# A two-layer decoder on one Trainium2 core: expert pieces of 896 columns, and expert rows given back by an indirect DMA

## Chip, cores and metric

The kernel runs on one core of a Trainium2 chip. The metric is the device time of one execution in microseconds; beside it the profiler gives the span of one profiled execution, from its first to its last instruction. The engines are TensorE (PE), VectorE (DVE), ScalarE (ACT), GpSimd (POOL) and SyncE (SP, which here only issues DMAs).

## What is computed

256 tokens of width 1024 go through two layers and a final RMSNorm, all in float32.

```python
for i in range(2):
    h = rmsnorm(x, norm_mix[i])                 # layer 0: S5 scan + GLU; layer 1: RWKV-7
    ca = memory_cross_attn(q, rmsnorm(mem, norm_mem[i]), w_kv_mem[i])
    x = x + concat([mix, ca]) @ w_out[i]
    h2 = rmsnorm(x, norm_ffn[i])
    x = x + (swiglu(h2, ...) if i == 0 else moe_swiglu(h2, ...))
return rmsnorm(x, norm_final)
```

The change concerns `moe_swiglu`, which takes about six tenths of the time. Each token picks its two best of eight experts; an expert is `(silu(h @ w_gate) * (h @ w_up)) @ w_down` with 1024 x 3584, 1024 x 3584 and 3584 x 1024 weights; its rows are scaled by the softmax weight of the choice and added to the token. Every expert's weights are read once: 8 x 44 MB of the 423 MB that the kernel moves.

## The kernel before, in words

**Products.** A float32 product is made of three fp32r products (`mm3`, L191 to L195): high part of x by high part of w, high by low, low by high. Each weight tile is therefore split on the chip (`split`, L173): ACT casts it to its high part (L187), DVE subtracts that to get the low part (L188), into a pool of four pairs (`ws`). The first expert's first pieces have their subtraction on GpSimd (L185).

**Weights.** `wload` (L119) fills a ring of seven tiles of 128 x 4096 floats, all through SP's queue (L63) in the order in which they are used. A tile is loaded again when its last split is done.

**Order.** The kernel writes its operations in program order and a scheduler places them on each engine by a simulated timeline; each engine, and SP's queue, then runs its list strictly in that order. A DMA that waits holds up every later DMA of SP.

**Experts.** Tokens are packed per expert into at most 128 rows; a second pass for fuller experts stands in a branch (L1757 to L1759) that these inputs don't take. `Gather` (L1445) builds a one-hot matrix `Gm` (tokens x rows) and gets the expert's rows by matmuls (L1458), turns them to columns (`xe`), and `back` (L1473) turns `Gm` into `GT` and fetches each row's weight and rstd (`wsl`). An expert's 3584 columns are cut into seven pieces of 512, so there are 56 jobs (expert, piece). A job runs 48 gate products into one PSUM tile `gu` of 128 x 512 (L193 to L195), then `between`: the previous job's activation is transposed and split (`act_T`, `ath` L1658 and `atl` L1659), and a finished expert is combined; then 48 up products, Silu on ACT (L1649) and the product with up on DVE (L1650). At piece 3 the next expert's rows are gathered. Last the previous job's down product runs, 24 products into two PSUM tiles `yac` that stay for the whole expert.

**Combine** (L1677). ACT scales `yac` by the rows' weights into a high part (L1685), DVE makes the low part (L1686), eight 128 x 512 products with `GT` (L1691, L1692) spread the rows to the tokens, and DVE adds them to the residual stream `xs` (L1696). For the last expert the adds go through `resid` (L269, L270), which also sums the squares for the final norm.

**Start.** The S5 stage loads its parameters (`bnat`, `cnat`, `gnat`) by SP among w_in_a's and mem's loads; PE transposes c (L507), ACT copies it (L514), makes U and Um (L537, L540) and the block columns BC (L501).

**End.** After the branch: `rstd_of` (L276 to L278), the scaling by rs and the gain `nfin` (L1766), and four stores. `nfin` was loaded on ACT's queue ahead of the experts (L1624 to L1626).

## Time and profile before

| | |
|---|---|
| median of 3 runs | 1589.86 us (1589.8 to 1590.88) |
| the profiled execution: time, span | 1590.0 us, 1588.0 us |
| mean granted clock of PE | 0.978 |
| busy: PE, DVE, ACT, POOL | 1516.3, 1283.0, 1073.0, 157.7 us |
| DMA packets, bytes | 198031, 423.46 MB |
| first gate product of the experts | 589.59 us |
| last down product | 1572.86 us |

How to read it: a row of the groups gives line, engine, operation, output tile and inputs, shapes and count, then busy time and mean nanoseconds of one, then the engine's idle time before it and what ended that. A row of the timeline gives start, duration, and in brackets the idle time before it. A row of the waits says who waited for whom, how long in total, how often, and the longest. Successive matmuls overlap in the profile, so that the distance of their starts, and not their duration, is what one costs in a stream. PSUM tiles and weight tiles carry the program's names.

### The profile page before, as it was taken

The page shows a single profiled execution, that of the slowest core. Times are in us where ns is not written, and L with a number is a line of the kernel's source. Part 1 is how long each engine was busy: PE and PEld are TensorE (multiplying, and loading weights), DVE is VectorE, ACT ScalarE, POOL GpSimd, SP SyncE. Part 2 cuts the span into 40 slices and gives each one's busy share as a digit, 9 for nine tenths or more (in the row PEclk, how much of TensorE's full clock was granted, in tenths as well). Part 3 has the DMA queues.
Part 4 walks back from the last instruction along what each step waited for, and adds up shares of the span by engine and source line. Part 5 has one row for each costly group of instructions (what it writes and reads, how often), then busy time and mean ns, then how long its engine had stood idle before and what let it go on. Part 6 is the DMA issues. An engine that isn't in the chain of part 4 may idle for free. (4 is left out here: it accounts for less than half of the span.)

```text
span 1588.0 us, 21853 instructions
## 1 busy us (share of the span) xinstructions
PE 1516.3 (95%) x8465; PEld 1272.1 (80%) x8465; DVE 1283.0 (81%) x1583; ACT 1073.0 (68%) x1355; POOL 157.7 (10%) x215
## 2 busy tenths in 40 slices
PE   7898999998969889999999999999999999999996
PEld 6776888878958768888888888888888888888885
DVE  7964654546895669899899899899899898988987
ACT  6655544436533348788777777787787887777775
POOL 3451000003652230000000000000000000000000
PEclk9999999999989979999999999999999999999999
DMA  7116553623400958999999999999999999999970
GB/s 202 45 45 237 185 203 117 248 79 94 120 14 22 339 218 313 341 371 359 346 374 353 344 376 356 340 378 356 347 372 363 348 366 361 352 348 366 360 280 29
DMA packets 198031, 423.46 MB, mean 267 GB/s; under 512 B 13952, under 2 KB 35614, under 8 KB 197918
## 3 DMA queue, kind: packets, MB, share of 16 engines
q1 hardware_dynamic: 195746, 419.29, 72.8%
q10 hardware_dynamic: 2172, 2.68, 0.6%
q8 instruction: 68, 1.11, 0.3%
q14 instruction: 45, 0.37, 0.1%
HBM read 420.91 MB, written 1.05 MB: 266 GB/s over the span
## 5 line engine op out<-in xcount | busy, mean ns | idle before, releaser
L188 DVE TENSOR_TENSOR wsl<-w,wsh 128x1024 fp32r<-128x1024 f32 (+1 forms) x757 | 893.8, 1216 | 150.9 <-ACT wsh L187 139.8
L187 ACT CAST wsh<-w 128x1024 fp32r<-128x1024 f32 (+1 forms) x757 | 783.3, 1049 | 250.9 <-PE gu L195 97.1
L194 PE MATMUL gu<-wsl,xeh 128*128 128x512 f32 x896 | 350.7, 391 | 0.0
L193 PE MATMUL gu<-wsh,xeh 128*128 128x512 f32 x896 | 348.9, 396 | 1.6 <-DVE xs L1696 1.6
L195 PE MATMUL gu<-wsh,xel 128*128 128x512 f32 x896 | 349.5, 390 | 0.0
L193 PEld LDWEIGHTS gu<-wsh,xeh 128*128 128x128 f32 x896 | 168.8, 188 | 37.4 <-ACT wsh L187 2.4
L195 PEld LDWEIGHTS gu<-wsh,xel 128*128 128x128 f32 x896 | 168.6, 188 | 35.1 <-DVE xel L1471 0.2
L194 PEld LDWEIGHTS gu<-wsl,xeh 128*128 128x128 f32 x896 | 168.7, 188 | 35.0
L194 PE MATMUL yac<-wsl,ath 128*128 128x512 f32 x440 | 173.0, 393 | 0.0
L195 PE MATMUL yac<-wsh,atl 128*128 128x512 f32 x440 | 171.7, 390 | 0.0
L193 PE MATMUL yac<-wsh,ath 128*128 128x512 f32 x440 | 136.3, 391 | 0.0
L278 POOL TENSOR_TENSOR rs<-vv,mhalf 128x1 f32<-128x1 f32 x8 | 4.4, 557 | 1203.6 <-DVE vv L277 1203.6
L195 PEld LDWEIGHTS yac<-wsh,atl 128*128 128x128 f32 x440 | 82.7, 188 | 17.1
L193 PEld LDWEIGHTS yac<-wsh,ath 128*128 128x128 f32 x440 | 82.2, 188 | 16.9
L194 PEld LDWEIGHTS yac<-wsl,ath 128*128 128x128 f32 x440 | 82.8, 188 | 15.4
L193 PE MATMUL mm<-wsh,hTh 128*128 128x512 f32 (+1 forms) x192 | 71.1, 374 | 0.0
L194 PE MATMUL mm<-wsl,hTh 128*128 128x512 f32 (+1 forms) x192 | 70.8, 371 | 0.0
L195 PE MATMUL mm<-wsh,hTl 128*128 128x512 f32 (+1 forms) x192 | 70.3, 372 | 0.0
L1658 ACT CAST ath<-t 128x512 fp32r<-128x512 f32 x55 | 32.3, 587 | 31.0 <-PE yac L194 30.2
L1650 DVE TENSOR_TENSOR sg<-sg,gu 128x512 f32<-128x512 f32 x56 | 38.1, 681 | 13.7 <-PE gu L195 13.7
L195 PE MATMUL dn<-hTh,wsC 128*128 128x256 f32 x160 | 46.5, 291 | 1.0 <-POOL wsC L1148 0.9
L193 PE MATMUL dn<-hTh,wsC 128*128 128x256 f32 x160 | 46.1, 288 | 0.0
(533 smaller groups left out, 2059.1 us busy)
## 6 DMA issues: line engine op xcount, KB each, us to landing
w<-in_moe_w_gate_dram SPq DMA_DIRECT2D x55, 2048.0 KB
w<-in_moe_w_up_dram SPq DMA_DIRECT2D x55, 2048.0 KB
w<-in_moe_w_down_dram SPq DMA_DIRECT2D x54, 2048.0 KB
w<-in_w_in_b_dram SPq DMA_DIRECT2D x22, 512.0 KB
w<-in_ffn_w_gate_dram SPq DMA_DIRECT2D x5, 2048.0 KB
w<-in_ffn_w_up_dram SPq DMA_DIRECT2D x5, 2048.0 KB
w<-in_ffn_w_down_dram SPq DMA_DIRECT2D x5, 2048.0 KB
w<-in_w_out_dram SPq DMA_DIRECT2D x4, 2048.0 KB
```

The costliest lines, as they stand in the source:

```text
L187: S.copy(hv, src)
L188: (eng or V).tensor_sub(lv, src, hv.bitcast(F32))
L193: TE.matmul(ps, xp[0], wh, start=start, stop=False, skip_group_check=True)
L194: TE.matmul(ps, xp[0], wl, start=False, stop=False, skip_group_check=True)
L195: TE.matmul(ps, xp[1], wh, start=False, stop=stop, skip_group_check=True)
L278: hold.append(G.tensor_tensor(rs, vv, mhalf, op=OP.pow).ins)
L1650: V.tensor_mul(sg, sg, ps[1])
L1658: S.copy(at[0], t)
```

## The change

**Expert pieces.** 896 columns in place of 512, so four pieces an expert and 32 jobs. Gate and up are loaded as two tiles of 128 x 4 x 896 each, down as one of four and one of three rows of 1024; runs in memory are 3584 bytes for gate and up (2048 before) and 4096 for down as before. Gate and up run in two halves of 448 columns, each with its own PSUM tile, so a job takes all four `gu` tiles; Silu, product and transposes follow those shapes, with one `sg` tile in place of two. The next expert's rows are gathered at piece 2.

**Giving back.** For the first seven experts ACT scales both halves of `yac` into one tile `ye`, and GpSimd scatters its 128 rows by an indirect DMA into a scratch `yd` in device memory: 512 rows, one for each token and rank of choice. The row number comes with the weights as a third column of `wt`, read in `back`; rows that hold no token fall outside and are skipped. GT, its transposes and the eight products remain for the last expert alone. During the last expert four reads of `yd`, each into `ye`, and four adds to `xs` on DVE (`added`) bring the rows in. `ye` has one buffer, also used for the gathered rows and by the last combine. `yd` is zeroed at the start by four DMAs from a cleared tile.

**Final norm.** `nfin` is loaded into a ring tile on ACT's queue after the branch.

**What moves.** On SP at the start, before (waits in brackets, `_49` belongs to the semaphores' names):

```order
L63 DMA srow2_111<-in_s5_d_dram 6x128 [waits DMAHW2_49]
L63 DMA srow2_111<-in_s5_b_glu_dram 6x128 [waits DMAHW3_49]
L63 DMA bnat_143<-in_s5_b_re_dram 128x24x16 [waits DMAHW4_49]
L63 DMA bnat_143<-in_s5_b_im_dram 128x24x16 [waits DMAHW5_49]
L63 DMA cnat_300<-in_s5_c_re_dram 128x6x64 [waits DMAHW6_49]
L63 DMA cnat_300<-in_s5_c_im_dram 128x6x64 [waits DMAHW7_49]
L63 DMA gnat_104<-in_s5_w_glu_dram 128x6x16 [waits DMAHW0_49]
```

and now:

```order
L63 DMA srow2_113<-in_s5_d_dram 6x128 [waits DMAHW2_49]
L63 DMA srow2_113<-in_s5_b_glu_dram 6x128 [waits DMAHW3_49]
L63 DMA yd_67<-KD_105 128x1024 [waits DMAHW4_49,Pool_49]
L63 DMA yd_67<-KD_105 128x1024 [waits DMAHW5_49]
L63 DMA yd_67<-KD_105 128x1024 [waits DMAHW6_49]
L63 DMA yd_67<-KD_105 128x1024 [waits DMAHW7_49]
L63 DMA bnat_149<-in_s5_b_re_dram 128x24x16 [waits DMAHW0_49]
L63 DMA bnat_149<-in_s5_b_im_dram 128x24x16 [waits DMAHW1_49]
L63 DMA cnat_306<-in_s5_c_re_dram 128x6x64 [waits DMAHW2_49]
L63 DMA cnat_306<-in_s5_c_im_dram 128x6x64 [waits DMAHW3_49]
L63 DMA gnat_106<-in_s5_w_glu_dram 128x6x16 [waits DMAHW4_49]
```

The four writes of zeros, which wait for GpSimd's clearing, stand ahead of every parameter of S5.

On DVE at the end, from the splits of the last down tile to the first residual add, before (`wsl` is the low part of a split, `w_22117` the last weight tile):

```order
L188 TENSOR_TENSOR wsl_22108<-w_21969,wsh_22107 128x1024 [waits DMAHW7_49,Activation_49]
L188 TENSOR_TENSOR wsl_22123<-w_22117,wsh_22122 128x1024 [waits DMAHW0_49,Activation_49]
L188 TENSOR_TENSOR wsl_22127<-w_22117,wsh_22126 128x1024 [waits DMAHW1_49,Activation_49]
L188 TENSOR_TENSOR wsl_22131<-w_22117,wsh_22130 128x1024 [waits DMAHW2_49,Activation_49]
L1659 TENSOR_TENSOR xel_22074<-t_22068,xeh_22073 128x512 [waits Activation_49]
L188 TENSOR_TENSOR wsl_22135<-w_22117,wsh_22134 128x1024 [waits DMAHW3_49,Activation_49]
L1686 SCALAR_TENSOR_TENSOR yel_22163<-yac_21357,wsl_20631,yeh_22162 128x512 [waits Activation_49]
L1686 SCALAR_TENSOR_TENSOR atl_22167<-yac_21358,wsl_20631,ath_22166 128x512 [waits Activation_49]
L269 TENSOR_TENSOR xs_72<-xs_72,gu_22170 128x512 [waits PE_49]
```

and now (`w_14226` and `w_14231` are the last two weight tiles, `yac_13584` the first half):

```order
L189 TENSOR_TENSOR wsl_14256<-w_14226,wsh_14255 128x1024 [waits DMAHW1_49,Activation_49]
L189 TENSOR_TENSOR wsl_14266<-w_14226,wsh_14265 128x1024 [waits DMAHW2_49,Activation_49]
L1655 TENSOR_TENSOR xs_74<-xs_74,ye_13581 128x1024 [waits DMAHW3_49]
L189 TENSOR_TENSOR wsl_14276<-w_14231,wsh_14275 128x1024 [waits DMAHW4_49,Activation_49]
L189 TENSOR_TENSOR wsl_14280<-w_14231,wsh_14279 128x1024 [waits DMAHW5_49,Activation_49]
L189 TENSOR_TENSOR wsl_14284<-w_14231,wsh_14283 128x1024 [waits DMAHW6_49,Activation_49]
L1655 TENSOR_TENSOR xs_74<-xs_74,ye_13852 128x1024 [waits DMAHW7_49]
L1726 SCALAR_TENSOR_TENSOR atl_14309<-yac_13585,wsl_12770,ath_14308 128x512 [waits Activation_49]
L1655 TENSOR_TENSOR xs_74<-xs_74,ye_13855 128x1024 [waits DMAHW0_49,DVE_49]
L1726 SCALAR_TENSOR_TENSOR ye_14305<-yac_13584,wsl_12770,ye_14305 128x512 [waits DMASW6_49,Activation_49]
L270 TENSOR_TENSOR xs_74<-xs_74,gu_14317 128x512 [waits PE_49]
```

The last three of the four adds (the rows onto `xs_74` from a `ye`) now stand among the last splits and ahead of the scaling of each half; the first stands 32 rows earlier.

On SP at the same place, now:

```order
L63 DMA w_14226<-in_moe_w_down_dram 128x1024 [waits DMAHW1_49]
L63 DMA w_14226<-in_moe_w_down_dram 128x1024 [waits DMAHW2_49]
L63 DMA ye_13581<-yd_67 128x1024 [waits DMAHW3_49,DVE_49]
L63 DMA w_14231<-in_moe_w_down_dram 128x1024 [waits DMAHW4_49,DVE_49]
L63 DMA w_14231<-in_moe_w_down_dram 128x1024 [waits DMAHW5_49]
L63 DMA w_14231<-in_moe_w_down_dram 128x1024 [waits DMAHW6_49]
L63 DMA ye_13852<-yd_67 128x1024 [waits DMAHW7_49,DMAHW3_49,DVE_49]
L63 DMA ye_13855<-yd_67 128x1024 [waits DMAHW7_49,DMAHW0_49,DVE_49]
L1802 COMPARE_AND_BRANCH
```

The third and the fourth read each wait for DVE, that is for the add before, since all go into the one `ye`; before, the last row here ahead of the branch was a load of weights.

The diff:

```diff
-    pad(consts, 64)
...
+    dr = pool(ctx, "dr", 1, space=bass.MemoryType.DRAM)
+    yd = dr.tile([2 * T, D], F32, name="yd")
...
+        for i in range(2 * NH):
+            dma(yd[i * P:(i + 1) * P, :], KD_[:, 0:2].rearrange("p q d c -> p (q d c)"))
...
-    wt = mcon.tile([P, NH, E, 2], F32, name="wt")
+    wt = mcon.tile([P, NH, E, 4], F32, name="wt")
+    tok = mcon.tile([P, NH], F32, name="tok")
...
+    pad(mcon, 96)
     class Gather:
...
-        def back(self, tr):
-
-            self.GT = self.mp.tile([P, NH, P], F32R, name="GT")
+        def back(self, tr, turned):
+
...
+            if turned:
+                self.GT = self.mp.tile([P, NH, P], F32R, name="GT")
+                for h in range(NH):
+                    TE.transpose(t[:, h, :], self.Gm[:, h, :].bitcast(F32), ident)
...
-                TE.transpose(t[:, h, :], self.Gm[:, h, :].bitcast(F32), ident)
-            for h in range(NH):
-                TE.matmul(t[:, 2, 0:2], self.Gm[:, h, :].bitcast(F32), wt[:, h, e, :], start=h == 0, stop=h == NH - 1,
+                TE.matmul(t[:, 2, 0:3], self.Gm[:, h, :].bitcast(F32), wt[:, h, e, 0:3], start=h == 0, stop=h == NH - 1,
...
-            S.copy(self.GT, t[:, 0:2, :])
+            if turned:
+                S.copy(self.GT, t[:, 0:2, :])
...
+            self.place = smk([P, 1], I32, "it")
+            V.tensor_scalar(self.place, t[:, 2, 2:3], 2.0 * T, None, op0=OP.add)
...
+        G.iota(tok, pattern=[[P, NH]], base=0, channel_multiplier=1, allow_small_or_imprecise_dtypes=True)
...
+        V.tensor_scalar(wt[:, :, :, 2], rkk, float(T), -2.0 * T, op0=OP.mult, op1=OP.add)
+        V.tensor_add(wt[:, :, :, 2], wt[:, :, :, 2], tok[:, :, None].to_broadcast([P, NH, E]))
...
-    NCK = FE // 512
+    CW = 896
+    NCK, KW, HW = FE // CW, CW // P, CW // 2
     def tr():
...
     def gu():
...
-    nfin = mp.tile([P, D], F32, name="nfin", bufs=1)
-    ap = a["norm_final"]
-    dma(nfin, bass.AP(tensor=ap.tensor, offset=ap.offset, ap=[[0, P], [1, D]]), S)
+    def ye_tile():
+        return mp.tile([P, D], F32R, name="ye", tag="ye", bufs=1)
+
+    def halved(t):
+        return lambda q: t[:, q * 512:(q + 1) * 512].bitcast(F32)
     def gather(e, base):
...
-        g.columns(lambda q: mp.tile([P, 512], F32R, name="xr", tag="ye" + "hl"[q], bufs=1).bitcast(F32))
-        g.back(tr)
+        g.columns(halved(ye_tile()))
+        g.back(tr, base > 0 or e == E - 1)
...
+
+    def added(k, h):
+
+        b = ye_tile().bitcast(F32)
+        dma(b, yd[k * T + h * P:k * T + (h + 1) * P, :])
+        V.tensor_add(xs[:, h, :], xs[:, h, :], b)
     def gate_up(g, w_in, between, first):
...
-            w = w_in[nm]
-            p_ = gu()
-            for wh, wl, k0 in split(ws, w, 4, last=hold if first and nm == "gate" else None):
-                for j in range(2):
-                    k = k0 + j
-                    mm3(p_, (g.xe[0][:, k, :], g.xe[1][:, k, :]), wh[:, j, :], wl[:, j, :], k == 0, k == KD - 1)
-            ps.append(p_)
+            ps += [gu() for _ in range(2)]
+            for i, w in enumerate(w_in[nm]):
+                for wh, wl, k0 in split(ws, w, 4, last=hold if first and nm == "gate" and i == 0 else None):
+                    k = 4 * i + k0
+                    for n in range(2):
+                        ns = slice(n * HW, (n + 1) * HW)
+                        mm3(ps[-2 + n][:, :HW], (g.xe[0][:, k, :], g.xe[1][:, k, :]), wh[:, 0, ns], wl[:, 0, ns], k == 0,
+                            k == KD - 1)
...
-        sg = mp.tile([P, 512], F32, name="sg")
-        S.activation(sg, ps[0], AF.Silu, scale=g.rs)
-        V.tensor_mul(sg, sg, ps[1])
+        sg = mp.tile([P, CW], F32, name="sg", bufs=1)
+        for n in range(2):
+            ns = slice(n * HW, (n + 1) * HW)
+            S.activation(sg[:, ns], ps[n][:, :HW], AF.Silu, scale=g.rs)
+            V.tensor_mul(sg[:, ns], sg[:, ns], ps[2 + n][:, :HW])
...
     def act_T(sg, pl):
-        t = tr()
-        for j in range(4):
-            TE.transpose(t[:, j, :], sg[:, j * P:(j + 1) * P], ident)
-        at = mkpair(pl, [P, 4, P], "at", 1) if pl is mp else tuple(v[:, 0:4] for v in mkpair(pl, [P, KD, P], "xe"))
-        S.copy(at[0], t)
-        V.tensor_sub(at[1], t, at[0].bitcast(F32))
+        at = mkpair(pl, [P, KW, P], "at", 1) if pl is mp else tuple(v[:, 0:KW] for v in mkpair(pl, [P, KD, P], "xe"))
+        for j0 in range(0, KW, 4):
+            js = slice(j0, min(j0 + 4, KW))
+            t = tr()[:, :js.stop - j0]
+            for j in range(j0, js.stop):
+                TE.transpose(t[:, j - j0, :], sg[:, j * P:(j + 1) * P], ident)
+            S.copy(at[0][:, js], t)
+            V.tensor_sub(at[1][:, js], t, at[0][:, js].bitcast(F32))
...
     def down(c, at, w, yac, end):
         def piece(wh, wl, k, n):
...
-                c == NCK - 1 and k == 3)
-        if not end:
-            for wh, wl, k in split(ws, w, 4):
+                c == NCK - 1 and k == KW - 1)
+        for i, w_ in enumerate(w):
+            k_ = w_.shape[1]
+            ps = ((wh, wl, 4 * i + k0) for wh, wl, k0 in split(ws, w_, k_, size=k_ * D))
+            if not (end and i):
+                for p_ in ps:
+                    for n in range(2):
+                        piece(*p_, n)
+            else:
+                ps = list(ps)
...
-                    piece(wh, wl, k, n)
-        else:
-            ps = list(split(ws, w, 4))
+                    for p_ in ps:
+                        piece(*p_, n)
+
+    def combine(yac, g, last, base):
+
+        ys = [None, None]
+        if not (base or last):
+            y = ye_tile().bitcast(F32)
...
-                for p_ in ps:
-                    piece(*p_, n)
-
-    def combine(yac, g, last):
-
-        ys = [None, None]
+                S.activation(y[:, n * 512:(n + 1) * 512], yac[n], AF.Copy, scale=g.w)
+            G.indirect_dma_start(yd[:, :], bass.IndirectOffsetOnAxis(g.place, 0), y, None, bounds_check=2 * T - 1,
+                                 oob_is_err=False)
+            return
         def scaled(n):
-            yh, yl = ys[n] = mkpair(mp, [P, 512], "ye", 1) if n == 0 or not last else mkpair(mp, [P, 4, P], "at", 1)
+            if n == 0 or not last:
+                y = ye_tile()
+                yh, yl = ys[n] = y[:, 0:512], y[:, 512:D]
+            else:
+                yh, yl = ys[n] = tuple(v[:, 0:4] for v in mkpair(mp, [P, KW, P], "at", 1))
...
         def w_down(e, c, cut):
-            return wload(4, D, (0, a["moe_w_down"][0, e][c * 512:(c + 1) * 512, :]), size=4096, cut=cut)
+            return [wload(k_, D, (0, a["moe_w_down"][0, e][c * CW + k0 * P:c * CW + (k0 + k_) * P, :]), size=4096,
+                          cut=k_ if cut else 1) for k0, k_ in ((0, 4), (4, KW - 4))]
         def finish(pd, at, w):
...
         for e, c in jobs:
-            cs = slice(c * 512, (c + 1) * 512)
+            cs = slice(c * CW, (c + 1) * CW)
...
-            cut = 4 if end else 1
-            w_in = {nm: wload(KD, 512, (0, a["moe_w_" + nm][0, e][:, cs]), size=4096, cut=cut)
-                    for nm in ("gate", "up")}
+            cut = 4 if end else 0
+            w_in = {nm: [wload(4, CW, (0, a["moe_w_" + nm][0, e][k0 * P:(k0 + 4) * P, cs]), size=4096, cut=cut or 1)
+                         for k0 in (0, 4)] for nm in ("gate", "up")}
...
             def between(pend=pend, first=base + e + c == 0):
...
-                    info[0].back(tr)
+                    info[0].back(tr, False)
                 if pend:
...
-                    combine(yacs[e_], info[e_], False)
+                    combine(yacs[e_], info[e_], False, base)
             sg = gate_up(info[e], w_in, between, base + e + c == 0)
...
-            if c == 3 and e + 1 < E:
+            if c == 2 and e + 1 < E:
...
+            if e == E - 1 and not base and 1 <= c < 1 + NH:
+                for k in range(2):
+                    added(k, c - 1)
             if pend:
...
-        combine(yacs[E - 1], info[E - 1], True)
+        combine(yacs[E - 1], info[E - 1], True, base)
...
+    ap = a["norm_final"]
+    nfin = wload(1, D, size=4096)[:, 0]
+    dma(nfin, bass.AP(tensor=ap.tensor, offset=ap.offset, ap=[[0, P], [1, D]]), S)
```

## The prediction, made before the run

> **What bounds the kernel now.** I read the busy times first, then the expert phase as one window, then the groups of instructions, the waits, and the timeline at the three places that the change touches outside the experts (start, last combine, final norm). The page says that TensorE (PE) is the fullest engine, and the window over the eight experts that it is full throughout.
>
> ```profile
> PE 1516.3 (95%) x8465; PEld 1272.1 (80%) x8465; DVE 1283.0 (81%) x1583; ACT 1073.0 (68%) x1355; POOL 157.7 (10%) x215
> ```
>
> ```profile
> core 0: us, PE busy (x) PEld busy (x) DVE busy (x) ACT busy (x) POOL busy (x), PEclk, DMA share, GB/s
> 590.00:1573.00 983.00, 981.23 (x4472) 810.46 (x4471) 892.83 (x860) 775.33 (x833) 0.00 (x0) 1.00 0.93 342
> ```
>
> PE is busy for 981 of 983 us at the full granted clock, VectorE (DVE) for 91%, ScalarE (ACT) for 79%, the DMA engines for 93%. Busy PE can hide short stalls, so the waits decide who leads:
>
> ```profile
> SPq L63 <- DVE wsl L188: 1034.2, 178, 26.2
> ACT wsh L187 <- PE gu L195: 97.1, 251, 2.2
> ```
>
> The DMA queue waits for DVE to free a weight tile (1034 us in all), and ACT waits for PE to free a split pair (97 us). No row has an expert's weights as what is waited for. So supply is ahead and PE sets the pace: 983 / 8 = 122.9 us an expert. What the change does to the experts' time is what it does to PE there; wider DMA runs alone buy nothing. Start and tail are chains of their own.
>
> **Part 1, PE work in the experts.** Two widths show what a product costs, start to start:
>
> ```profile
> 998.99 0.39 PE L193 MATMUL gu<-wsh,xeh 128*128 128x512 f32 x1
> ...
> 1000.12 0.39 PE L195 MATMUL gu<-wsh,xel 128*128 128x512 f32 x1
> ```
>
> ```profile
> 398.97 0.28 PE L194 MATMUL dn<-hTl,wsC 128*128 128x256 f32 x1
> ...
> 399.68 0.28 PE L194 MATMUL dn<-hTl,wsC 128*128 128x256 f32 x1
> ```
>
> Five steps in 1.13 us make 0.226 us for 512 columns; six steps in 0.71 us make 0.118 us for 256. A line through both gives 0.226 - 64 x 0.108 / 256 = 0.199 us for 448. Gate and up take 56 x 2 x 8 x 3 = 2688 products now and 32 x 2 x 8 x 2 x 3 = 3072 after (more steps, each narrower): 3072 x 0.199 - 2688 x 0.226 = **+4 us**. The ends are 0 (cost in proportion to columns) and +87 (no cheaper than 512 columns); two measured points on a line make me take +4. The Trainium skill, "TensorE: Matmul & The Clock Gate", section "Back-to-back issue gap", has a fixed 2.5 ns beside the columns at full clock; by it the edit costs about +1 us, and its 215.8 ns for 512 is below the 226 that the trace shows, so the trace's line stands.
>
> Seven of eight experts lose the eight 128x512 products that give their rows back: 56 x 0.226 = **-12.7 us**. They also lose two transposes each:
>
> ```profile
> 1565.70 0.60 PE L1656 MATMUL t<-ident,sg 128*128 128x128 f32 x4
> 1566.06 0.48 PE L194 MATMUL yac<-wsl,ath 128*128 128x512 f32 x1
> L193 PE MATMUL gu<-wsh,xeh 128*128 128x512 f32 x896 | 348.9, 396 | 1.6 <-DVE xs L1696 1.6
> ```
>
> Four transposes move the next product by 0.36 us and last 0.60, so 14 are worth 1.3 to 2.1; I take **-1.5**. The third row is the only stall after a combine that the groups show: gate products that waited 1.6 us for the adds to free a PSUM tile; those adds go, **-1.6**. The down products stay. Sum on PE: 4 - 12.7 - 1.5 - 1.6 = **-11.8 us**.
>
> Cover: nothing may become later than PE. DVE's rows:
>
> ```profile
> L188 DVE TENSOR_TENSOR wsl<-w,wsh 128x1024 fp32r<-128x1024 f32 x749 | 888.3, 1221 | 140.6 <-ACT wsh L187 129.4
> L188 DVE TENSOR_TENSOR wsl<-w,wsh 128x512 fp32r<-128x512 f32 x8 | 5.5, 691 | 10.4 <-ACT wsh L187 10.4
> L1686 DVE SCALAR_TENSOR_TENSOR yel<-yac,wsl,yeh 128x512 fp32r<-128x512 f32 x15 | 11.2, 747 | 4.0 <-ACT yeh L1685 4.0
> L1696 DVE TENSOR_TENSOR xs<-xs,gu 128x512 f32<-128x512 f32 x28 | 18.1, 680 | 2.0 <-PE gu L1692 2.0
> ```
>
> A split of 896 columns lies on the line at 1.089 us; 512 of them and 224 of 1.221 are 831 us against 672 x 1.221 = 821: +10. Gone are 14 x 0.747 + 28 x 0.680 = 29.5. The four adds are priced as a split of their size (4 x 1.22 = 4.9). The Silu products in other shapes add 2 or 3. DVE falls by about 12 us, so PE keeps its lead; if that cover went, each microsecond of DVE would count once. On ACT, casts of 896 columns cost about 12 us more and the GT copies go: still near 80%.
>
> **Part 2, the start.** Four writes of 512 KB that zero the scratch stand on SP ahead of the S5 inputs; behind them wait b, c, the GLU weights, further w_in_a and mem, and so the transposes of c, and ACT.
>
> ```profile
> DMA  0048999996999979999999999910100089899943
> DMA packets 966, 3.48 MB, mean 348 GB/s; under 512 B 115, under 2 KB 115, under 8 KB 964
> q1 hardware_dynamic: 964, 3.47, 88.7%
> 18.29 1.34 ACT L514 ACTIVATE cT<-trp 64x192 f32<-64x192 f32 x4 [2.09 <-PE trp L507]
> 26.68 4.90 ACT L540 COPY Um<-U 32x128 f32<-32x128 f32 x16
> 31.60 2.54 ACT L501 COPY BC<-m 64x512 f32<-64x512 f32 x4
> DVE m L497 <- ACT BC L501: 4.9, 3, 2.5
> ```
>
> The first row is the DMA share from 0 to 30 us in steps of 0.75: nearly full from 2.3 to 19 us, so the zeros push what follows. The next two are the queue from 1530 to 1540 us: 3.47 MB in 8.87 us of full engines, hence 5.4 us for 2.1 MB. ACT's chain begins 2.09 us after a wait for the c transposes and runs without a gap to the BC copies, for which DVE then waits. A push of 5.4 us at its head is partly filled, since U and Um there need no c. Bounds: 0 and +6 (the push and SP's four issues); I take **+3**.
>
> **Part 3, the tail.** The reads of the scratch and their adds share one tile, so the third read waits for the second add, which the order puts behind four splits of the last down tile, and the fourth for the third. ACT's scaling of the first half waits for the fourth add, as it reuses the tile.
>
> ```profile
> 1568.35 1.22 DVE L188 TENSOR_TENSOR wsl<-w,wsh 128x1024 fp32r<-128x1024 f32 x1
> 1572.86 0.39 PE L195 MATMUL yac<-wsh,xel 128*128 128x512 f32 x1
> 1572.83 0.69 ACT L1685 ACTIVATE yeh<-yac,wsl 128x512 fp32r<-128x512 f32 x1 [4.52 <-PE yac L195]
> 1573.56 0.75 DVE L1686 SCALAR_TENSOR_TENSOR yel<-yac,wsl,yeh 128x512 fp32r<-128x512 f32 x1 [3.98 <-ACT yeh L1685]
> 1575.39 1.88 DVE L269 TENSOR_TENSOR xs<-xs,gu 128x512 f32<-128x512 f32 x3 [0.42 <-PE gu L1692]
> ```
>
> Now the last split ends 3.3 us before the last down product starts, and the residual adds begin 2.5 us after that. After: the last tile has three rows, whose last pair is first needed 12 products, 2.7 us, before the end (15 and 3.4 now, as these rows have it). Add two stands ahead of the last three splits (3 x 1.22) and so ends some 6 us before the last product; its read comes back in about 3.5 us (next part), add three ends near 0.9 us before the last product, the fourth read is back at +2.6 and added by +3.9; scaling 0.69 and 0.75 bring the residual adds to about +5.5. That is **+3 us** against +2.5 now; bounds 0 (the pause holds both reads) and +5 (reads take 4.5 us each).
>
> **Part 4, the final norm.** Its gain is no longer read before the experts, but on ACT's queue behind the branch.
>
> ```profile
> L63 ACTq DMA_DIRECT2D nfin<-in_norm_final_dram x1: 334/334/334, 572.7 to 572.7; - x1
> DMA  0000000000000000698889997554121000000000
> 1580.97 0.23 DVE L276 TENSOR_TENSOR vv<-ssq 128x1 f32<-128x1 f32 x2 [3.10 <-ACTq L1758]
> 1581.98 2.74 DVE L1766 SCALAR_TENSOR_TENSOR xs<-xs,rs,nfin 128x512 f32<-128x512 f32 x4 [0.59 <-POOL rs L278]
> ```
>
> The second row is that load alone from 572 to 577 us in steps of 0.125: issued at 572.7, its packets run from 574.0 to 575.9, so 3.2 us, and some tenths until the semaphore. ACT leaves the branch at about 1580.95. Issued then, the gain is there near 1584.9, and DVE, which starts at 1581.98, waits **+3 us** (bounds +2.2 and +4.5). The routing gains two DVE operations of under 0.2 us: **+0.3**.
>
> **Sum**, from the profiled execution's 1590.0 us (span 1588.0 and 2.0 outside it): -11.8 + 3 + 3 + 3 + 0.3 = -2.5, hence 1587.5. The median of the runs is 1589.9, so this execution stands for them. What a measurement of this kernel can tell from no change is about 0.2%, 3.2 us; -2.4 us against the median lies within it.
>
> **Rivals.** *A, faster: the start is hidden and PE's small losses go.* ACT and DVE fill the wait for c, part 2 costs 0, the tail 1, and DVE's 12 us turn into 2 us fewer stalls: 1590.0 - 11.8 - 2 + 1 + 3 + 0.3 = 1580.5. For it: U and Um can move ahead. Against it: ACT's chain had no gap, and PE is busy 981 of 983 us already.
>
> *B, slower: the scatters hold DVE.* Each of seven experts now has GpSimd write out 128 row addresses in the midst of DVE's splits, where GpSimd was idle (0.00 in the window). The nearest rows have GpSimd beside DVE:
>
> ```profile
> 576.08 7.03 POOL L185 TENSOR_TENSOR wsl<-w,wsh 128x1024 fp32r<-128x1024 f32 x3
> 578.40 0.21 DVE L1552 TENSOR_TENSOR g<-lgt 128x64 f32<-128x64 f32 x1
> 578.53 2.36 DVE L1553 TENSOR_TENSOR e<-lgt 128x64 f32<-128x64 f32 x1
> ```
>
> Two operations of one size on DVE, and one lasts 2.15 us longer while a GpSimd subtraction runs. If a scatter held DVE for that once, 7 x 2.15 = 15 us, at worst all of it PE's: 1602.5; half of it 1595. It decides from about 1.4 us on, PE's work on one pair (six products), since the four pairs are rarely all full. Against it: a scatter writes few bytes into SBUF, unlike a 128x1024 subtraction. The Trainium skill, "GPSIMD Engine Reference", section "Key points", has GpSimd share its SBUF interfaces with VectorE and contend with instructions of two SBUF inputs, which every split is; its rule would make this rival true, and no run here shows a scatter.
>
> *C, slower: start and tail both at their upper ends*, +6, +5, +4.5 and +0.3 against -11.8: 1594. For it: all three are chains in which nothing else is due.
>
> *D, the runs of 3584 bytes don't pay.* An expert is 8192 packets of 3584 bytes and 3584 of 4096 now. In part 2's queue rows some 849 packets of 4096 bytes took 16 engines 8.87 us, at most 167 ns each, in proportion 146 for 3584: (8192 x 146 + 3584 x 167) / 16 = 112 us, below PE's 121.4. DMA leads only if the shorter packet costs over 164; if it costs the same 167, an expert takes 122.9 us as now, 12 us more than forecast, 1599.5.
>
> **How the numbers follow.** The forecast, 1587.5 with a range of its own from 1584 to 1591.5, has a chance of 0.44; A 0.28; B 0.12; C 0.12; D 0.04. The range leaves out D, B at its full price and A's far edge: 1579 to 1597. Faster by over 0.2% (below 1586.7): A and 0.13 of the forecast, 0.41. Within 0.2% (to 1593.0): the rest of the forecast, 0.31, and 0.04 of C. Slower: 0.08 of C, B and D, 0.24.
>
> **What would show it.** PE's stretch from the first gate product to the last down product is shorter by 11 to 13 us, with gate products 0.199 us apart; if not, part 1 is wrong. The BC copies begin near 34.6 us and everything up to the experts is later by about 3. The residual adds begin 5 to 6 us after the last product, and the final scaling waits 3 us for the gain. DVE operations of over 2 us beside a scatter would show B; a weight DMA as a releaser, D. A measured time outside 1584 to 1591.5 means that one of these four terms is mis-sized.

## The result, and the profile after

After: 1609.95 us, the median of 4 runs (1609.65 to 1610.95). Before, on the same chip: 1590.37 us (1589.8 to 1591.15). The ratio is 1.0124, with a 95% interval from 1.0106 to 1.0141: slower by 20 us, where the forecast was 1587.5 and the range ended at 1597. One of the ten executions of e4 below took 3057.98 us, the others 1587.22 to 1594.77, and e4's ratio leaves that one out.

The two profiled executions, cut at the points that the prediction named (starts of the first gate product, last down product, first residual add and final scaling):

| stretch, us | before | after | change | forecast |
|---|---|---|---|---|
| start to first gate product | 589.59 | 593.01 | +3.4 | +3.3 |
| to the last down product (experts) | 983.27 | 992.47 | **+9.2** | **-11.8** |
| to the first residual add | 2.53 | 5.82 | +3.3 | +3 |
| to the final scaling | 6.59 | 10.74 | +4.2 | +3 |
| to the end | 6.04 | 5.97 | -0.1 | 0 |

Everything outside the experts came as forecast, within 1.2 us (for the start this may be luck, as said below at part 2). The experts missed by 21 us. The busy times of after (the page's first part) say nothing of it; DVE even fell by 11 us:

```profile
PE 1520.9 (95%) x8779; PEld 1334.1 (83%) x8779; DVE 1271.9 (79%) x1635; ACT 1079.4 (67%) x1426; POOL 162.0 (10%) x223
```

The windows of after show two kinds of experts, an early and a late stretch of 100 us each (columns as in the prediction's window):

```profile
800.00:900.00 100.00, 100.00 (x488) 89.55 (x487) 91.30 (x93) 80.96 (x94) 1.09 (x1) 1.00 0.97 368
1100.00:1200.00 100.00, 98.95 (x481) 86.95 (x480) 88.34 (x93) 78.82 (x91) 1.10 (x1) 1.00 0.93 349
```

The clock is 1.00 in both, but in the later one PE has 1.05 us of idle time, and DVE and the DMA engines do less. The scatters mark the experts, one at the end of each. GpSimd's timeline of after:

```profile
741.07 1.35 POOL L1713 DMA_INDIRECT yd<-ye,it  x1 [154.59 <-ACT ye L1712]
863.69 1.09 POOL L1713 DMA_INDIRECT yd<-ye,it  x1 [121.28 <-ACT ye L1712]
985.88 1.10 POOL L1713 DMA_INDIRECT yd<-ye,it  x1 [121.10 <-ACT ye L1712]
1111.33 1.10 POOL L1713 DMA_INDIRECT yd<-ye,it  x1 [124.34 <-ACT ye L1712]
1236.75 1.10 POOL L1713 DMA_INDIRECT yd<-ye,it  x1 [124.33 <-ACT ye L1712]
```

The distances are 122.6, 122.2, 125.5 and 125.4 us an expert, where 121.4 was forecast: one loss in all experts, and 3 us more from the fourth on. The waits of after name what is new. `sg` L1674 (L1650 in before) is the Silu product, in which DVE multiplies the Silu of gate by the up products; it has to wait until PE has finished the up products. Before's row for this wait stands behind the three of after:

```profile
DVE sg L1674 <- PE gu L196: 35.3, 16, 2.4
PEld t L1683 <- DVE sg L1674: 9.4, 15, 0.7
PE yac L195 <- DVE wsl L189: 3.3, 14, 0.5
```

```profile
DVE sg L1650 <- PE gu L195: 13.7, 11, 1.6
```

Here is one late job of after: the end of the up products on PE, then DVE, then ACT.

```profile
1127.58 0.36 PE L196 MATMUL gu<-wsh,xel 128*128 128x448 f32 x1
1128.26 0.55 PE L1683 MATMUL t<-ident,sg 128*128 128x128 f32 x3 [0.32 <-DVE sg L1674]
1128.56 0.71 PE L194 MATMUL yac<-wsh,ath 128*128 128x512 f32 x2
1129.11 0.60 PE L1683 MATMUL t<-ident,sg 128*128 128x128 f32 x4
1129.92 0.50 PE L195 MATMUL yac<-wsl,ath 128*128 128x512 f32 x1 [0.21 <-DVE wsl L189]
```

```profile
1127.58 1.15 DVE L1674 TENSOR_TENSOR sg<-sg,gu 128x448 f32<-128x448 f32 x2 [2.39 <-PE gu L196]
1128.65 5.76 DVE L189 TENSOR_TENSOR wsl<-w,wsh 128x1024 fp32r<-128x1024 f32 x5
```

```profile
1124.34 1.05 ACT L188 CAST wsh<-w 128x1024 fp32r<-128x1024 f32 x1 [0.27 <-PE gu L196]
1125.55 1.05 ACT L188 CAST wsh<-w 128x1024 fp32r<-128x1024 f32 x1 [0.16 <-PE gu L196]
```

ACT's first cast for the down products is done at 1125.39, and from there on DVE could subtract. But the next operation on its list is the Silu product, and DVE stands 2.39 us until the up products end. Then the two Silu products go first and five splits follow in a row. PE, which used to find splits waiting, starts the transposes 0.68 us after its last up product (0.20 is a full step), and then waits 0.21 us for its first `wsl`. In an early job of after there is no such wait:

```profile
817.70 3.67 DVE L189 TENSOR_TENSOR wsl<-w,wsh 128x1024 fp32r<-128x1024 f32 x3 [0.20 <-ACT wsh L188]
821.28 1.15 DVE L1674 TENSOR_TENSOR sg<-sg,gu 128x448 f32<-128x448 f32 x2
822.34 4.62 DVE L189 TENSOR_TENSOR wsl<-w,wsh 128x1024 fp32r<-128x1024 f32 x4
```

Three of the seven down splits stand ahead of the Silu products here. The order of the changed kernel on DVE has it so in jobs 2 to 12, except those that gather rows. In job 13 one stands ahead, and in jobs 14 to 31 none, again except those that gather: 14 jobs, as many as the waits of `yac` for `wsl`. The order of before has three of four ahead in its first 40 jobs and one to three in the others. The Silu products of job 14 in the order of after, between its last up split and its first down split:

```
L189 TENSOR_TENSOR wsl_9116<-w_8934,wsh_9115 128x896 [waits Activation_49]
L1674 TENSOR_TENSOR sg_9125<-sg_9125,gu_9043 128x448 [waits PE_49]
L1674 TENSOR_TENSOR sg_9125<-sg_9125,gu_9044 128x448 [waits PE_49]
L189 TENSOR_TENSOR wsl_9133<-w_8936,wsh_9132 128x1024 [waits DMAHW7_49,Activation_49]
```

PE's time in the expert stretch by kind of product, from each start to the next one's, summed over the trace (us; e5 is an experiment below):

| | before | forecast change | after | e5 |
|---|---|---|---|---|
| gate and up | 618.2 | +4 | 632.0 (+13.8) | 626.0 (+7.8) |
| down | 308.4 | 0 | 312.0 (+3.6) | 311.0 (+2.6) |
| transposes of the activation | 19.8 | 0 | 28.0 (+8.2) | 21.5 (+1.7) |
| products with GT, and the stall behind | 14.9 | -14.3 | 0 (-14.9) | 0 (-14.9) |
| the rest (gathering) | 22.0 | -1.5 | 20.5 (-1.5) | 20.5 (-1.5) |

The removals came as forecast. What was priced at nothing or little is what grew.

### The profile page after: what moved, and what is told of

Its sections match the earlier page's. It is cut to its first block, busy times and chain, and to the rows that moved or that the text cites. A ratio compares the mean times of both kernels' runs of the same rounds, so it can differ in the third digit from the quotient of the medians.

```text
span 1608.0 us, 22803 instructions
## 1 busy us (share of the span) xinstructions
PE 1520.9 (95%) x8779; PEld 1334.1 (83%) x8779; DVE 1271.9 (79%) x1635; ACT 1079.4 (67%) x1426; POOL 162.0 (10%) x223
## 5 line engine op out<-in xcount | busy, mean ns | idle before, releaser
L189 DVE TENSOR_TENSOR wsl<-w,wsh 128x896 fp32r<-128x896 f32 (+2 forms) x821 | 898.5, 1134 | 157.7 <-ACT wsh L188 145.9
L188 ACT CAST wsh<-w 128x896 fp32r<-128x896 f32 (+2 forms) x821 | 793.9, 983 | 266.5 <-PE yac L196 102.0
L195 PE MATMUL gu<-wsl,xeh 128*128 128x448 f32 x1024 | 376.1, 367 | 0.0
L196 PE MATMUL gu<-wsh,xel 128*128 128x448 f32 x1024 | 374.6, 366 | 0.0
L194 PE MATMUL gu<-wsh,xeh 128*128 128x448 f32 x1024 | 290.1, 366 | 0.0
L194 PEld LDWEIGHTS gu<-wsh,xeh 128*128 128x128 f32 x1024 | 192.4, 188 | 16.9 <-ACT xeh L1475 0.2
L195 PEld LDWEIGHTS gu<-wsl,xeh 128*128 128x128 f32 x1024 | 192.8, 188 | 16.5 <-DVE wsl L189 0.2
L196 PEld LDWEIGHTS gu<-wsh,xel 128*128 128x128 f32 x1024 | 192.6, 188 | 16.1 <-DVE xel L1476 0.2
L1674 DVE TENSOR_TENSOR sg<-sg,gu 128x448 f32<-128x448 f32 x64 | 37.4, 616 | 35.6 <-PE gu L196 35.3
L195 PE MATMUL dn<-hTl,wsC 128*128 128x256 f32 x160 | 45.7, 286 | 0.0
```

The costliest lines, as they stand in the source:

```text
L188: S.copy(hv, src)
L189: (eng or V).tensor_sub(lv, src, hv.bitcast(F32))
L194: TE.matmul(ps, xp[0], wh, start=start, stop=False, skip_group_check=True)
L195: TE.matmul(ps, xp[0], wl, start=False, stop=False, skip_group_check=True)
L196: TE.matmul(ps, xp[1], wh, start=False, stop=stop, skip_group_check=True)
L1674: V.tensor_mul(sg[:, ns], sg[:, ns], ps[2 + n][:, :HW])
```

## The experiments

The theory after the first look: two causes share the 21 us, the price of 448 columns on PE, and an order. The order was at first taken to be the place of the transposes on PE (e2); when e2 missed, the order on DVE took its place (e5). Rivals were that 448 columns cost more only beside the DMA traffic, and that giving the rows back by DMA saves nothing.

**e1, the width by itself.** PE streams products of one width after the other, with weights and inputs that stand in SBUF and nothing beside them.

```diff
+    for i, n in enumerate(WIDTHS):
+        ps = [pp.tile([P, 512], F32, name=f"ps{n}", tag="ps", bufs=4) for _ in range(2)]
...
+                TE.matmul(ps[j][:, :n], xh, wh[:, ms], start=r == 0, stop=False, skip_group_check=True)
+                TE.matmul(ps[j][:, :n], xh, wl[:, ms], start=False, stop=False, skip_group_check=True)
+                TE.matmul(ps[j][:, :n], xl, wh[:, ms], start=False, stop=r == REPS - 1, skip_group_check=True)
```

> This kernel leaves the whole model out: it only runs streams of 192 products on TensorE (fp32r, 128 rows, the same pattern of high and low parts as the experts) at widths 512, 448, 256, 384, 480, 416, 320, 512 and 448, with no other engine and no DMA beside them. Theory 'width' (a product of 448 columns costs more than the line through 256 and 512 says, by itself): 448 starts 0.2025 us apart here too, 512 0.2266, 256 0.118. Rival 'contention' (the 3 ns more per product come from the splits or the weight DMAs beside it): 448 starts 0.1995 apart here, on the line.

The windows of e1 for the last seven of its nine streams of 192 products (256, 384, 480, 416, 320, 512 and 448 columns; a count takes in a neighbour that is still running):

```profile
90.27:113.30 23.03, 23.03 (x193) 1.00 0.00 1
113.30:146.59 33.29, 33.29 (x194) 1.00 0.00 1
146.59:188.49 41.90, 41.90 (x193) 1.00 0.00 0
188.49:224.76 36.27, 36.27 (x193) 1.00 0.00 1
224.76:252.91 28.15, 28.15 (x193) 1.00 0.00 1
252.91:296.41 43.50, 43.50 (x194) 1.00 0.00 1
296.41:335.20 38.79, 38.79 (x193) 1.00 0.00 0
```

Divided by 192: 0.1199, 0.1734, 0.2182, 0.1889, 0.1466, 0.2266 and 0.2020 us; the mean step over all of e1's 448 products is 0.2026. 256, 320, 384 and 512 lie on a line (0.0267 us for each 64 columns), on which 448 would be 0.2000. 416, 448 and 480 lie above it, by 2 to 5 ns. No DMA runs (0.00), so traffic is not the cause. In after's trace a step in the 448 streams is 0.2027 us from 660 to 1600 us, the same. The forecast's 0.199 had two faults: its line went through 0.118 us for 256, read from six steps, where 256 costs 0.120, and it took 448 to lie on the line. With the full steps of the two traces, 0.20265 us in after and 0.22694 in before, the term is 3072 x 0.20265 - 2688 x 0.22694 = +12.5 us, not +4. The Trainium skill, "TensorE: Matmul & The Clock Gate", section "Back-to-back issue gap", has 2.5 ns beside the columns for an isolated product; the line through the streams leaves 2 x 0.1199 - 0.2266 = 13 ns at no columns, and the measurement decides. By the page's rule the edit would have cost about +1 us, an estimate.

**e2, the transposes held back.** After, with a job's transposes issued behind the last down product of the job before.

```diff
+            with tc.issue_after(tail_[0]) if tail_ and pl is mp else ExitStack():
+                for j in range(j0, js.stop):
+                    TE.transpose(t[:, j - j0, :], sg[:, j * P:(j + 1) * P], ident)
```

> The changed kernel with one thing undone: the transposes of a job's activation are held behind the last down product of the job before, where the program's order can't put them right behind the up products. Theory 'order' (15 jobs from the fourth expert on wait 0.47 us for the Silu product and another 0.46 us for the split of the transposed tile, 13 us in all): about 1597 to 1599, no stall of over 0.4 us between an up product and a transpose. Rival 'scatter' (GpSimd's scatters, their DMAs and the one shared tile slow the experts) and theory 'width' both expect no change from the order: 1610 within 2 us.

It took 1641.34 us, 1.0342 (1.0293 to 1.0392) of before: a miss by over 40 us. A wait of e2, and DVE and PE at a late job:

```profile
PE yac L195 <- DVE wsl L189: 22.5, 15, 1.5
```

```profile
1233.19 1.15 DVE L1674 TENSOR_TENSOR sg<-sg,gu 128x448 f32<-128x448 f32 x2 [2.39 <-PE gu L196]
1234.26 5.76 DVE L189 TENSOR_TENSOR wsl<-w,wsh 128x1024 fp32r<-128x1024 f32 x5
```

```profile
1233.20 0.36 PE L196 MATMUL gu<-wsh,xel 128*128 128x448 f32 x1
1233.40 0.63 PE L194 MATMUL yac<-wsh,ath 128*128 128x512 f32 x2
1235.54 0.50 PE L195 MATMUL yac<-wsl,ath 128*128 128x512 f32 x1 [1.51 <-DVE wsl L189]
```

DVE waits as in after, 2.39 us, and so its first down split comes as late; without the transposes to do meanwhile PE stands 1.5 us at each of 15 jobs. The transposes had filled part of the hole; their place was a symptom. By kinds, against after: down +21.2, transposes -6.3, and gate and up +11.7. About 6 of the 11.7 are the 448 streams, which run at 0.2047 us a step here (3072 x 0.002); why they do is open (end of the document), and the rest was not taken apart.

**e3, the pieces alone.** 896 columns, but rows given back by products with GT as before; no scratch, no zeroing, no reads of it. The gain is late as in after.

```diff
-            G.indirect_dma_start(yd[:, :], bass.IndirectOffsetOnAxis(g.place, 0), y, None, bounds_check=2 * T - 1,
-                                 oob_is_err=False)
-            return
...
-                for k in range(2):
-                    added(k, c - 1)
```

> The pieces of 896 alone: rows given back by products as before, no scratch, no zeroing, no reads; the final gain still loaded behind the branch. If width and order carry the loss: against before +4 for narrower products, +9 for their price, +7 for about eight jobs whose transposes stand right behind the up products, +3 for the gain, hence 1611 to 1615. If the scatter carries it: only +4 and +3, about 1597.

1615.29 us, 1.0143 (1.0126 to 1.016). The expert stretch takes 1004.05 us, 20.8 more than before's. That is the upper end of what width and order were expected to give without any scatter, so the scatter does not carry the loss. DVE waits for the up products in 8 jobs here, where it does so in 16 in after.

**e4, the giving back alone.** Pieces of 512 columns, everything else of the change.

```diff
-    CW = 896
-    NCK, KW, HW = FE // CW, CW // P, CW // 2
+    CW = 512
+    NCK, KW = FE // CW, CW // P
```

> The other half alone: pieces of 512 as before, rows given back by scatter, reads and adds, zeroing at the start, gain behind the branch. If width and order carry the loss: the experts become 14 to 16 us shorter than before, start +3.4 and end +7.4 as in the changed kernel, hence 1583 to 1587. If the scatter carries it: the experts are no shorter than before and the time is 1600 or more.

1590.43 us, 0.9989 (0.9978 to 1.0). The expert stretch is 967.02 us, 16.3 shorter than before's, where the forecast's three terms for this are 12.7 + 1.5 + 1.6 = 15.8. So the saving is real, and the start, the tail and the gain eat it. The total is still a miss, by 3 us above the expected range: the start is 5.6 us longer than before's, where 3.4 was expected, and the end 11.4, where 7.4 was. Its DVE timeline at the end shows the chain through the one `ye` in full:

```profile
1563.12 1.23 DVE L1655 TENSOR_TENSOR xs<-xs,ye 128x1024 f32<-128x1024 f32 x1 [3.15 <-DMA ye<-yd]
...
1567.95 1.23 DVE L1655 TENSOR_TENSOR xs<-xs,ye 128x1024 f32<-128x1024 f32 x1 [2.95 <-DMA ye<-yd]
```

Two reads of the scratch wait for an add each, and their adds end behind the last down product (1562.19): the residual adds begin 9.45 us after it, not 2.5.

**e5, only DVE's order.** After, with the two Silu products issued behind the first two splits of the next down tile.

```diff
-            V.tensor_mul(sg[:, ns], sg[:, ns], ps[2 + n][:, :HW])
-        return sg
+
+        def mul():
+            for n in range(2):
+                ns = slice(n * HW, (n + 1) * HW)
+                V.tensor_mul(sg[:, ns], sg[:, ns], ps[2 + n][:, :HW])
+        return sg, mul
...
+                    if mul and i == 0 and p_[2] == 1:
+                        with tc.issue_after(lows[0]):
+                            mul()
```

> The changed kernel with one order undone on VectorE: the two products of Silu with up (L1674) are issued behind the first two splits of the down tile that comes next, and no longer ahead of them. Theory 'DVE order' (DVE waits 16 times 2.4 us for the last up product while down splits whose high parts are ready stand behind it; TensorE then has nothing to multiply): DVE's 35 us of waits for the up products go, TensorE's stalls at the transposes and at the first low part go, 1597 to 1599. Rival 'supply' (DVE and ACT can't keep up with pieces of 896 whatever the order): 1606 to 1610, with the waits elsewhere.

1597.18 us, 1.0037 (1.0024 to 1.0049). The work is that of after, operation by operation, and the expert stretch falls from 992.47 to 978.91 us. DVE and the scatters in e5:

```profile
1125.41 2.44 DVE L189 TENSOR_TENSOR wsl<-w,wsh 128x1024 fp32r<-128x1024 f32 x2 [0.23 <-ACT wsh L188]
1127.77 1.14 DVE L1678 TENSOR_TENSOR sg<-sg,gu 128x448 f32<-128x448 f32 x2
1128.83 4.62 DVE L189 TENSOR_TENSOR wsl<-w,wsh 128x1024 fp32r<-128x1024 f32 x4
```

```profile
1111.32 1.10 POOL L1720 DMA_INDIRECT yd<-ye,it  x1 [121.36 <-ACT ye L1719]
1233.79 1.10 POOL L1720 DMA_INDIRECT yd<-ye,it  x1 [121.38 <-ACT ye L1719]
```

Two splits fill what was the wait, the products follow without idle time, and a late expert takes 122.5 us like an early one, not 125.4. DVE's order is shown as the cause of 13.6 us.

**e6, e5 with gate and up cut 512 + 384.** Both widths lie on e1's line, so a pair should be cheaper than two of 448.

```diff
+        cut_ = (slice(0, 512), slice(512, CW))
...
-                        ns = slice(n * HW, (n + 1) * HW)
+                        ns = cut_[n]
```

> As the run before, and gate and up are cut into 512 and 384 columns in place of 448 and 448: as many products, but of the two widths that lie on the line when measured alone (0.2267 and 0.1734 us, mean 0.2000, against 0.2026). Theory 'width': 3072 x 0.0026 = 8 us less than the run before, 1589 to 1591. If the price of 448 columns alone were not what the model pays: no change from the run before, 1597 to 1599.

1605.8 us, 1.009 (1.0074 to 1.0107): slower than e5 by 8.6 us, a miss. The profiled execution is a long one, 1626.68 us, with the experts beginning only at 613.5; its expert stretch of 989.37 us is 10.5 longer than e5's. e1 had run each width by itself; e6 mixes them, mostly in the order 512, 384, 512, 512, 384, 384. Hence the next one.

**e8, widths in alternation.** The streams of e1 again, with two widths or two columns to start from in turn.

```diff
+    for g, cols, turn in GROUPS:
+        ps = [(pp.tile([P, 512], F32, name="ps" + g, tag="ps", bufs=4), c) for c in cols]
```

> Leaves the whole model out again: streams of 96 or 192 products on TensorE alone, told apart by the PSUM tile's letter. A: 448 columns always from column 0. B: 448 from column 0 and 448 in turn, three products each. C: 448 from column 0 and 512 in turn. D: as B, but changing after each product. E: 512 from 0 and 512, changing after each. F: 512 from 0 and 384 from 512, three each. G: as F, changing after each product. H: 384 from 0 and 512, changing after each. I: 416 from 0 and 416. If where the columns start sets the price: A and C 0.200, B and D over it. If the width itself: A to D all 0.2026. If a change of width costs: F and G above the mean of 0.2267 and 0.1734, which is 0.2000, near the 0.2076 that the run with uneven halves had, G more than F; E and H on 0.2267 and 0.1734.

The timeline of e8 in the stream that alternates 512 and 384, two products a row:

```profile
249.33 0.58 PE L79 MATMUL psG<-wh,xh 128*128 128x512 f32 x2
249.74 0.57 PE L79 MATMUL psG<-wl,xh 128*128 128x512 f32 x2
```

A pair takes 0.413 us on the mean of the stream: 0.237 for the 512 and 0.176 for the 384, where each by itself costs 0.227 and 0.173. With three of one width and then three of the other it is 0.408. e6's own trace, whose order is neither, has full steps of 0.2353 and 0.1769 from 660 to 1600 us, 0.412 a pair, and two of 448 take 0.405 in e5. So 1536 pairs cost about 10 us more, which is what e6 loses against e5. Where in the tile the columns start made no difference to 448 (0.2067 at 0 and at 448), but that is 4 ns more than the same stream took in e1, and neither of the two prices that were expected.

**e9 and e10, the start and the gain alone.** e9 is before with only the scratch and its four zeroing DMAs; e10 is before with only the gain's load moved behind the branch.

```diff
+        for i in range(2 * NH):
+            dma(yd[i * P:(i + 1) * P, :], KD_[:, 0:2].rearrange("p q d c -> p (q d c)"))
```

> The kernel before with nothing added but the scratch and its four zeroing DMAs at the start, which nothing reads. If they push the S5 inputs as forecast: +3 against before (0 to +6), seen up to the first output product. If they are hidden: no change, and the later start of the experts in the changed kernel is TensorE's clock in the K and V products near 110 us, as in the run of the pieces alone, which had no zeroing and began its experts 3.1 us late with the same order of instructions.

```diff
-    nfin = mp.tile([P, D], F32, name="nfin", bufs=1)
...
+    nfin = wload(1, D, size=4096)[:, 0]
+    dma(nfin, bass.AP(tensor=ap.tensor, offset=ap.offset, ap=[[0, P], [1, D]]), S)
```

> The kernel before with one move: the final gain is loaded behind the branch, on ScalarE's queue, as in the changed kernel. As forecast the final scaling starts 3 us later and the time is +3 (bounds +2.2 and +4.5); by the changed kernel's trace, where 10.7 us lie between the first residual add and the final scaling against 6.6 before, +4.1.

e9 took 1596.51 us, 1.0034 (1.0017 to 1.005): +4.7. e10 took 1595.17, 1.0019 (1.0009 to 1.003): +3.3. ACT's wait for the transposes of c in after, and DVE's wait for the gain in after and in e10:

```profile
21.07 1.33 ACT L517 ACTIVATE cT<-trp 64x192 f32<-64x192 f32 x4 [5.28 <-PE trp L510]
32.93 2.52 ACT L504 COPY BC<-m 64x512 f32<-64x512 f32 x4
1602.04 2.74 DVE L1813 SCALAR_TENSOR_TENSOR xs<-xs,rs,w 128x512 f32<-128x512 f32 x4 [3.70 <-DMA w<-in_norm_final_dram]
```

```profile
1584.28 2.74 DVE L1765 SCALAR_TENSOR_TENSOR xs<-xs,rs,w 128x512 f32<-128x512 f32 x4 [3.72 <-DMA w<-in_norm_final_dram]
```

**e7, the part that pays.** Pieces of 512 and the giving back by scatter, with three changes that are meant to take its side costs away: the scratch is zeroed in the first expert's first job from a `ye` that GpSimd clears, the four reads go into one ring tile behind the last weights, so that none waits for an add, and the gain is loaded ahead of the experts as in before.

```diff
-        b = ye_tile().bitcast(F32)
-        dma(b, yd[k * T + h * P:k * T + (h + 1) * P, :])
+        b = ring["w"].tile([P, 4096], F32, name="w", tag="w")
...
+            if base + e + c == 0:
+                y = ye_tile().bitcast(F32)
+                G.memset(y, 0.0)
+                for i in range(2 * NH):
+                    dma(yd[i * P:(i + 1) * P, :], y)
```

> Pieces of 512 with the scatter, and the three costs outside the experts taken away: the scratch is zeroed in the first expert's first job from a tile that GpSimd clears, the four reads go into one free weight tile behind the last weights, so that none waits for an add, and the final gain is read ahead of the experts as before. If start, reads and gain are what eats the scatter's gain: experts 16 us shorter than before, the residual adds 2.5 to 3 us after the last down product, the final scaling 6.6 us after those, 1573 to 1577 against 1590 for before on the same chip. If the gain is lost in another way (the adds on DVE, the zeroing beside the weights): 1582 or more.

1573.31 us, 0.9897 (0.9879 to 0.9914) of before: it beats both kernels. Its first gate product is at 589.72 us, the expert stretch takes 964.94, and DVE at the end has no wait for the scratch:

```profile
1552.35 3.49 DVE L1661 TENSOR_TENSOR xs<-xs,w 128x1024 f32<-128x1024 f32 x3
...
1557.18 2.48 DVE L270 TENSOR_TENSOR xs<-xs,gu 128x512 f32<-128x512 f32 x4
```

The residual adds begin 2.5 us after the last down product (1554.66), as in before. One row of e7's waits limits how after's may be read:

```profile
DVE sg L1677 <- PE gu L196: 39.8, 29, 1.6
```

DVE waits for the up products longer in sum than in after (35.3 us), and yet e7 is the fastest kernel here. No wait of PE for a split or for `sg` stands in its list, which after has for both. So it is PE's waits behind DVE's that cost time, and DVE's wait alone is no sign of a loss.

## Why the prediction was wrong

**What bounds the kernel: right.** PE set the pace in both kernels, and no weight DMA appears as what an expert waits for, so packets of 3584 bytes did not set the time (rival D). Wider runs brought no gain that shows: e3 has them and is slower.

**Part 1 failed, in two of its steps.** First, "two measured points on a line make me take +4": 448 columns cost 0.2027 us, not 0.199, which is +12.5 in the stream. The prediction's own bounds (0 to +87) held this, but its range took almost nothing of them in. Second, and larger, the cover: "DVE falls by about 12 us, so PE keeps its lead". DVE did fall by 11 us. But the sentence added up DVE's work and did not look at the order in which DVE has to do it. Before, one Silu product a job stood behind one to three down splits; after, two stand ahead of all seven in 14 jobs, so that DVE waits for PE while splits are ready, and then PE waits for DVE. That is 13.6 us by e5, and it could be read before the run: the order showed no down split ahead of L1674 in those jobs. Of the miss of 21.0 us, 13.6 are DVE's order; the other 7.4 stand in e5's column: gate and up 3.8 over the forecast, down 2.6, transposes 1.7, less 0.6 saved beyond it. The width's +12.5 is partly offset there by shorter gaps between the streams: before's gate and up took 8 us more than 2688 full steps, e5's 3 us more than 3072. The 2.6 and 1.7 were not taken further apart. The terms -12.7, -1.5 and -1.6 were right (e4: -16.3 for all three).

**Part 2 met its number, but its way holds only in part.** The c transposes are late (ACT waits 5.28 us, not 2.09), as said, and the start is 3.4 us longer. But the BC copies begin at 32.93, only 1.3 us later than before and not near 34.6, since U and Um went ahead of them. Further on PE waits for ACT's `xh`, in before and in after:

```profile
68.63 1.09 PE L555 MATMUL trp<-ident,xh 128*128 128x128 f32 x8 [0.42 <-ACT xh L550]
```

```profile
72.61 1.97 PE L558 MATMUL trp<-ident,xh 128*128 128x128 f32 x8 [4.26 <-ACT xh L553]
```

The mean granted clock from 40 to 160 us is also lower, 0.91 against 0.94. e3, which zeroes nothing, has 0.91 there as well and begins its experts 3.1 us late. Zeroing alone does cost time (+4.7 by e9's medians, interval 2.7 to 8.0, with a clock of 0.90 there). How much of after's 3.4 is the push and how much the clock stays open, so that they met the forecast's +3 may be luck.

**Part 3 right.** +3.3 for +3; the third and fourth read wait for an add each, as said. That one `ye` is the cause is shown by e7, where a tile of its own for all four gives 2.5 us.

**Part 4 right.** DVE waits 3.70 us for the gain, where it waited 0.59 for `rs` before; +3.3 by e10's medians. The stretch as a whole grew by 4.2; the other 1.1 was not traced.

**Rivals.** B, scatters that hold DVE, did not come. A scatter takes GpSimd 1.1 us (1.35 the first; its timeline above). The 14 DVE splits that run beside the seven scatters last 1.091 to 1.093 us each, and the median of all 480 of their size is 1.091. Those around the fourth, at 1111.33:

```profile
1110.49 1.09 DVE L189 TENSOR_TENSOR wsl<-w,wsh 128x896 fp32r<-128x896 f32 x1
1111.91 2.09 DVE L189 TENSOR_TENSOR wsl<-w,wsh 128x896 fp32r<-128x896 f32 x2 [0.33 <-ACT wsh L188]
```

The rule of the Trainium skill, "GPSIMD Engine Reference", section "Key points", that GpSimd contends with VectorE instructions of two SBUF inputs, is not borne out for these scatters. A and C moved only the terms outside the experts, where nothing was wrong. No rival had the mechanism that decided, an operation at the wrong place in DVE's list, though DVE at 91% of the stretch was the engine nearest to the limit.

## What to carry to other kernels

When an engine that feeds the bound is near 90% busy, its order has to be read as well as its sum: look in its list for operations that wait for the bound engine, count the ready work queued behind each, and do so along the whole stage, since a scheduler can place them otherwise from some job on. Whether such a wait costs anything is told by the waits of the bound engine right behind it. Price a matmul width that the kernel does not have yet by a stream of that width in the mix in which it will run, not by a line between others. A change made of several parts is worth taking apart: here one part was worth 1% by itself once its side costs were removed, and another cost as much.

## What the hardware showed that was not expected

- The step of an fp32r product is not linear in its columns: 416, 448 and 480 cost 0.189, 0.203 and 0.218 us by themselves, 2 to 5 ns above the line of 256, 320, 384 and 512; and 512 and 384 in turn cost 0.413 a pair in e8, not 0.400.
- The same width has more than one price: 448 columns take 0.2026 us a step in e1, 0.2027 in after and e5, 0.2047 in e2 and 0.2067 in e8, each at the full granted clock. What sets it stays open.
- The granted clock can drop for some us early in the program and shift all that follows. From 110 to 116 us e3 has 0.50 where before, with the same operations in the same order there, has 1.00; its experts start 3.1 us later. So the profiled starts of two kernels can differ by 3 us without a cause in the edit. The windows of before and of e3:

```profile
110.00:116.00 6.00, 5.88 (x31) 5.20 (x31) 2.74 (x6) 1.43 (x4) 5.14 (x5) 1.00 0.00 0
```

```profile
110.00:116.00 6.00, 5.43 (x15) 4.32 (x15) 2.96 (x7) 1.91 (x6) 5.62 (x6) 0.50 0.00 0
```
